# Two row-tile weighings moved from SBUF slots to PSUM banks, and a finer last product, in a fast matrix multiplication

## The chip, the cores and the metric

One core of one Trainium2 chip. The metric is device time in microseconds (us), the median over the executions of one kernel; 2% is the limit for calling two kernels different.

## The reference

```python
x: (8, 2048, 2048) float32      w: (2048, 2048) float32
cs   = np.cumsum(x, axis=1)
diff = cs - (cs shifted by one row, zero in front)      # = x again
return np.matmul(diff, w).astype(np.float32)
```

The differences of a running sum are x itself, so the work is one product of 16384 x 2048 by 2048 x 2048.

## The kernel before

The kernel takes four tiles of 128 rows as a group and saves matmuls by multiplying sums of blocks (Strassen's and Winograd's idea, on two levels), in fp16. Before it is narrowed to fp16, each row is *weighed*: ScalarE (ACT) sums the absolute values of the row, VectorE (DVE) makes a scale of the sum (`scale_of`), ACT narrows the row with it (`ready`), and a DMA transposes it (`turn`). TensorE (PE) accumulates products in PSUM; V, X, Y and Z are pairs of the eight banks ([128, 512] f32 each) that the kernel allocates there. ACT evicts a product to a slot of the SBUF pool C (`keep`) or DVE adds it to one (`add`); `put` stores a slot, 512 KB.

The ACTIVATE that sums also writes its elementwise result (128x2048 into c at L105, 128x512 into b at L553 in the profile below), which nobody needs. `weigh` lets it fall into a free slot of C; `weigh_in` into two idle PSUM banks, 512 columns at a time:

```python
def product(ps, a, b, first):        # 16 matmuls of 512 columns, L468
def product_in(ps, a, b, first):     # 4 matmuls, L479

def keep(dst, ps, scale):            # ACT, L497
    for c, p in pieces_of(dst, ps):
        after("act", lambda: nc.scalar.activation(c, p, COPY, scale=scale))

def add(dst, ps, scale):             # DVE, L502
    ...scalar_tensor_tensor(c, p, scale, c, MUL, ADD)

def weigh(t, slot):                  # one ACTIVATE of 2048 columns, L105
    xf = came.pop(t)
    m, _ = after("act", lambda: measure(xf, new_c(slot)))
    ...

def weigh_in(t, ps):                 # four ACTIVATEs of 512 columns, L553, and a reduce on DVE, L561
    for i in range(4):
        ...nc.scalar.activation(ps[i % 2], xf[:, ds(i * NB, NB)], ABS,
                                scale=1.0 / ROW, accum_out=m4[:, i : i + 1])
    after("dve", lambda: nc.vector.tensor_reduce(m, m4, AX.X, ADD))
```

`after` keeps the instructions of an engine in the order in which they were written. This is the end of the first group of this kind, and the start of the group after it (`second`), where the two weighings stand:

```python
def group_plain(g, X, Y, Z, V, a, b, c, d):   # the first group of this kind
    ...
    product(Z, S1, T1, True)
    ...
    weigh(h + 4, b); scale_of(h + 4); ready(h + 4); turn(h + 4)
    fetch_x(h + 5)
    weigh(g + 5, c)                # row tile 9
    scale_of(g + 5)
    C22 = new_c(d)
    keep(C22, Z, vh)               # TensorE needs this bank pair again
    product(X, A22g, T4, False)
    C21 = new_c(b)
    keep(C21, X, vg)
    ready(g + 5); turn(g + 5); put(C21, g + 1, 0)
    product(Y, A21h, T3, False)
    ...

def group(g, X, Y, Z, V, a, b, c, d):
    second = g == PLAIN + 4
    ...
    if second:
        product(X, A11g, B11, True)
    ...
    keep(C11g, X, ug)
    S3g = sums(g, S4g)
    if second:
        weigh(h + 1, c)            # row tile 11
        ready(h + 1)
        less_in(*in4)
    turn(h + 1)
    fetch_x(h + 4)
    product(Y, A11h, B11, True)
    if second:
        weigh_in(g + 4, V)
    keep(C11h, Y, uh)
    ...
```

The changed part of the end of the last group, `four_last`, stands in the diff.

Of the kernel before, what the change touches and what calls it, by code (L numbers as in the profile page):

```python
# [33 lines left out]
def kernel(  # L34
# [6 lines left out]
    nc = tc.nc  # L41
    P = 128
# [7 lines left out]
    NB = 512  # L50
# [18 lines left out]
    out2 = out.rearrange("b s d -> (b s) d")  # L69
# [23 lines left out]
    def bank(i):  # L93
        return psum.tile([P, NB], f32, name=f"b{i}")
# [8 lines left out]
    def measure(xf, waste):  # L103
        m = small.tile([P, 1], f32, name="m")
        return m, nc.scalar.activation(  # L105
            waste.bitcast(f16), xf, ABS, scale=1.0 / ROW, accum_out=m
        )
# [26 lines left out]
    def after(engine, ask):  # L134
        if engine in last:
            with tc.issue_after(last[engine].ins):
                said = ask()
        else:
            said = ask()
        last[engine] = said[-1] if isinstance(said, tuple) else said  # L140
        return said


    with tc.tile_pool(name="ring", bufs=7) as ring, tc.tile_pool(
# [81 lines left out]
        def here(h, r):  # L226
            return range(1 if h == 0 and r == PLAIN - 1 else 2)
# [14 lines left out]
        def put(c, rows, columns, queue=nc.gpsimd):  # L242
            return queue.dma_start(out2[rows, columns], c)
# [20 lines left out]
        ps = [[bank(2 * r + n) for n in here(0, r)] for r in range(PLAIN)]  # L264
# [10 lines left out]
        for ko in range(KO - KQ):  # L275
# [9 lines left out]
            if ko in turns:  # L285
                q, a = turns[ko]
# [19 lines left out]
        ps = [[bank(2 * r + n) for n in here(1, r)] for r in range(PLAIN)]  # L306
# [170 lines left out]
    def product_in(ps, a, b, first):  # L477
        for k in range(4):
            nc.tensor.matmul(  # L479
                ps, a[k], b[k], start=(first and k == 0), stop=(k == 3), skip_group_check=True  # L480
            )
# [8 lines left out]
    def pieces_of(dst, ps):  # L490
        if isinstance(ps, list):
            return [(dst[:, ds(n * NB, NB)], ps[n]) for n in range(2)]
        return [(dst, ps)]

    def keep(dst, ps, scale):
        for c, p in pieces_of(dst, ps):
            after("act", lambda: nc.scalar.activation(c, p, COPY, scale=scale))  # L497

    def add(dst, ps, scale):
        for c, p in pieces_of(dst, ps):  # L500
            after(
                "dve", lambda: nc.vector.scalar_tensor_tensor(c, p, scale, c, MUL, ADD)  # L502
            )
# [9 lines left out]
    def less(dst, p, q):  # L513
        for k in range(len(dst)):
            after("dve", lambda: nc.vector.tensor_tensor(dst[k], p[k], q[k], SUB))  # L515
# [10 lines left out]
    def new_c(slot):  # L526
        return cpool.tile([P, NH], f32, name=f"c{slot}")
# [9 lines left out]
    def weigh(t, slot):  # L537
        if t < END:
            xf = came.pop(t)
            m, _ = after("act", lambda: measure(xf, new_c(slot)))  # L540
            got[t] = m, None, xf


    def weigh_in(t, ps):
        if t < END:
            xf = came.pop(t)
            m = small.tile([P, 1], f32, name="m")
            m4 = small.tile([P, 4], f32, name="m4")
            for i in range(4):
                at = ds(i * NB, NB)  # L550
                after(
                    "act",
                    lambda: nc.scalar.activation(  # L553
                        ps[i % 2],
                        xf[:, at],
                        ABS,
                        scale=1.0 / ROW,
                        accum_out=m4[:, i : i + 1],
                    ),
                )  # L560
            after("dve", lambda: nc.vector.tensor_reduce(m, m4, AX.X, ADD))  # L561
            got[t] = m, None, xf
# [21 lines left out]
    def unit(t):  # L584
        u = small.tile([P, 1], f32, name="u")
        after("dve", lambda: nc.vector.tensor_scalar(u, got[t][0], uw, None, MUL))  # L586
        return u
# [59 lines left out]
    def group_plain(g, X, Y, Z, V, a, b, c, d):  # L647
        h = g + 2
        ug, uh = unit(g), unit(h)
        A11g, A12g = parts(g)  # L650
        A11h, A12h = parts(h)
        A21g, A22g = parts(g + 1)
        product(X, A11g, B11, True)
        for k in range(3):
            block(B22, 1, 1, k, "act")
        C11g = new_c(a)
        keep(C11g, X, ug)
        for k in range(3, KH):
            block(B22, 1, 1, k, "act" if k < 6 else "dve")
        product(V, A12g, B21, True)  # L660
        product(Y, A11h, B11, True)
        add(C11g, V, ug)
        put(C11g, g, 0)

        less(T3[:2], B22[:2], B12[:2])
        total(S1, A21g, A22g, ADD)
        product(Z, A12h, B21, True)
        weigh(h + 1, d)
        C11h = new_c(b)
        keep(C11h, Y, uh)  # L670
        total(S2, S1, A11g, SUB)
        less(T2[:4], B22[:4], T1[:4])
        scale_of(h + 1)
        vg = unit(g + 1)
# [3 lines that stand above are left out]
        less(T2[4:], B22[4:], T1[4:])  # L678
        product(V, S1, T1, True)
        C22 = new_c(d)  # L680
        keep(C22, V, vg)
        less(T3[2:3], B22[2:3], B12[2:3])
        total(S4g, A12g, S2, SUB)
        product(X, S2, T2, False)
        C12g = new_c(c)
        keep(C12g, X, ug)
        total(A21g, A11g, A21g, SUB)
        less(T3[3:], B22[3:], B12[3:])
        product(V, S4g, B22, False)
        A21h, A22h = parts(h + 1)  # L690
        vh = unit(h + 1)
        weigh(g + 4, a)
        product(X, A21g, T3, False)
        total(S1, A21h, A22h, ADD)
        total(S2, S1, A11h, SUB)
        add(C11h, Z, uh)
        put(C11h, h, 0)
        scale_of(g + 4)
        ready(g + 4)
        turn(g + 4)  # L700
        add(C12g, V, ug)
        put(C12g, g, 1)
        fetch_x(g + 5)
        product(Y, S2, T2, False)
        C12h = new_c(a)
        keep(C12h, Y, uh)
        add(C22, X, vg)
        put(C22, g + 1, 1)
        total(S4h, A12h, S2, SUB)
        less(T4, B21, T2)  # L710
        product(Z, S1, T1, True)
        total(A21h, A11h, A21h, SUB)
        weigh(h + 4, b)
        scale_of(h + 4)
        ready(h + 4)
        turn(h + 4)
        fetch_x(h + 5)
        weigh(g + 5, c)
        scale_of(g + 5)
        C22 = new_c(d)  # L720
        keep(C22, Z, vh)
# [3 lines that stand above are left out]
        ready(g + 5)  # L725
        turn(g + 5)
        put(C21, g + 1, 0)
        product(Y, A21h, T3, False)
        add(C22, Y, vh)
        put(C22, h + 1, 1)  # L730
        less_in(*in2)
        less_in3(*in2)
        product(Z, S4h, B22, False)
        add(C12h, Z, uh)
        put(C12h, h, 1)
        fetch_x(g + 8)
        less_in(*in3)
        product(Y, A22h, T4, False)
        C21 = new_c(c)
        keep(C21, Y, vh)  # L740
        put(C21, h + 1, 0)

    def group(g, X, Y, Z, V, a, b, c, d):
        h = g + 2
# [5 lines left out]
        q, e, y, z = banks  # L750
# [6 lines left out]
        keep(C11g, X, ug)  # L757
        S3g = sums(g, S4g)
        if second:
            weigh(h + 1, c)  # L760
            ready(h + 1)
            less_in(*in4)
        turn(h + 1)
# [9 lines left out]
        vg, vh = unit(g + 1), unit(h + 1)  # L773
# [4 lines left out]
        one, two, A2 = sums_in(A12g, A12h, S4h, S0)  # L778
# [34 lines left out]
        one, two, A3 = sums_in(S4g, S4h, S0, S3g)  # L813
# [11 lines left out]
        one, two, A4 = sums_in(A22g, A22h, S1, S2)  # L825
# [46 lines left out]
        def four_last():  # L872
            a11, a12, a22, s1, s2, s3, s4 = A4
            Q1, Q2, Q4, t11, Q3, t21, t22 = in4
            C21g, C21h = new_c(b), new_c(c)
            product_in(q, a11, t11, True)
            keep(C21g[:, :NB], q, vg)
            product_in(X[0], a12, t21, False)
            add(C21g[:, :NB], X[0], vg)
            product_in(X[1], s4, t22, False)  # L880
            keep(C21g[:, NB:], X[1], vg)
            product_in(e, s1, Q1, True)
            add(C21g[:, NB:], e, vg)
            keep(C21h[:, NB:], Y[1], vh)
            add(C21h[:, NB:], e, vh)
            product_in(q, s2, Q2, False)
            add(C21g[:, NB:], q, vg)
            put(C21g, g + 1, 0)
            product_in(Y[0], a22, Q4, False)
            keep(C21h[:, :NB], Y[0], vh)  # L890
            product_in(q, s3, Q3, False)
            for n in range(2):
                at = ds(n * NB, NB)
                add(C21h[:, at], q, vh)
                nc.scalar.dma_start(out2[ds((h + 1) * P, P), at], C21h[:, at])

        inner_product(A3, in3, banks, C12g, C12h, *u, between_3)
        put(C12h, h, 1)
# [9 lines left out]
    for g in range(PLAIN, END, 4):  # L908
        (group_plain if g == PLAIN else group)(g, *banks, *slots)
        a, b, c, d = slots  # L910
# [31 lines left out]
```

## Time and profile before

| | before |
|---|---|
| median of 3 executions (range), us | 1509.28 (1508.52 to 1510.85) |
| span of the profiled execution, us | 1507.3 |
| TensorE busy, us (matmuls) | 1490.6 (6911) |
| TensorE's waits for ACT at the first boundary, us | 1.32 + 0.20, later 0.78 |
| TensorE's wait for DVE at the end, us | 0.50 |

The prediction below shows the lines behind these numbers. Two more lines, from the page's table of the costliest groups, name the two ways of weighing. The columns: line, engine, operation, output and inputs with their shapes, count; then busy time in us and mean ns of one; then idle time just before them and what ended most of it.

```profile
L105 ACT ACTIVATE c<-fin 128x2048 f16<-128x2048 f32 x92 | 175.7, 1910 | 242.4 <-DMA out_dram<-c 220.5
...
L553 ACT ACTIVATE b<-fin 128x512 f32<-128x512 f32 x116 | 67.8, 585 | 14.5 <-DMA fin<-in_x_dram 14.5
```

The first line is the reason to try the change: 92 weighings into C stood idle for 220.5 us behind stores out of C. The second says what a weighing in PSUM waits for instead: nothing but the load of x.

### The profile page before, as it was taken

How to read it: one execution, taken by the hardware profiler on the slowest of the kernel's cores; microseconds unless marked ns; L12 is line 12 of the kernel's file. 1: busy time of each engine (PE TensorE's matmuls, PEld its weight loads, DVE VectorE, ACT ScalarE, POOL GpSimd, SP SyncE). 2: the span in 40 equal slices, each digit the busy share in tenths (PEclk: the TensorE clock that was granted, in tenths of full speed). 3: DMA queues.
4: the chain of work that ended last, by engine and by line, in shares of the span. 5: the costliest groups of instructions: out<-in, count | busy, mean ns of one | idle time of the engine just before them, and what ended most of it. 6: DMA issues, size and time to landing. Idle time of an engine off the chain costs nothing.

```text
span 1507.3 us, 19123 instructions
## 1 busy us (share of the span) xinstructions
PE 1490.6 (99%) x6911; PEld 673.8 (45%) x6911; DVE 1104.4 (73%) x2053; ACT 864.5 (57%) x1107; POOL 5.2 (0%) x12
## 2 busy tenths in 40 slices
PE   8999999999999999999999999999999999999998
PEld 3444444444444444444444444444444444444443
DVE  7997777776677676777676776766776767776767
ACT  5875655565655566555656555655555565556551
POOL 0100000000000000000000000000000000000000
PEclk9999999999999999999999999999999999999999
DMA  9988878878978987888789788878788888887772
GB/s 362 351 250 233 236 224 246 234 213 227 235 225 244 224 224 236 215 246 236 210 229 232 230 241 217 235 222 248 216 244 207 236 221 250 232 236 216 223 208 112
DMA packets 322479, 351.50 MB, mean 233 GB/s; under 512 B 266896, under 2 KB 266896, under 8 KB 306512
## 3 DMA queue, kind: packets, MB, share of 16 engines
q1 hardware_dynamic: 321536, 347.92, 81.1%
q0 software_dynamic: 560, 1.84, 0.3%
q8 instruction: 54, 0.88, 0.2%
q10 hardware_dynamic: 288, 0.52, 0.1%
q14 instruction: 41, 0.34, 0.1%
HBM read 150.99 MB, written 134.22 MB: 189 GB/s over the span
## 4 chain that ended last, share of the span: by engine, by line
PE 88%; DVE 1%; DMA 1%; issue 0%; ACT 0%; DVEq 0%; ACTq 0%; SPq 0%
PE b L468 52%; PE b L479 36%; DVE c L502 1%; DMA fin<-in_x_dram 0%; DMA xT<-fin 0%; DVE W L511 0%; ACT b L553 0%; DVE W L515 0%; ACT c L497 0%; DVEq L937 0%; DVE xT L511 0%; DVE s L112 0%; DVE m L111 0%; DVE u L586 0%; DVE m L561 0%
## 5 line engine op out<-in xcount | busy, mean ns | idle before, releaser
L502 DVE SCALAR_TENSOR_TENSOR c<-b,u,c 128x512 f32<-128x512 f32 (+1 forms) x883 | 675.0, 799 | 234.8 <-ACT c L497 112.8
L497 ACT ACTIVATE c<-b,u 128x512 f32<-128x512 f32 x496 | 314.5, 680 | 265.4 <-PE b L468 170.5
L468 PE MATMUL b<-W,xT 128*128 128x512 f16 x2048 | 462.1, 379 | 0.8 <-ACT c L497 0.8
L468 PE MATMUL b<-W,W 128*128 128x512 f16 x1764 | 411.7, 379 | 1.8 <-ACT c L497 1.5
L105 ACT ACTIVATE c<-fin 128x2048 f16<-128x2048 f32 x92 | 175.7, 1910 | 242.4 <-DMA out_dram<-c 220.5
L468 PEld LDWEIGHTS <-xT 128*128 128x128 f16 x2048 | 200.4, 98 | 242.6 <-issue 1.1
L468 PEld LDWEIGHTS <-W 128*128 128x128 f16 x2016 | 197.2, 98 | 240.2 <-issue 2.1
L116 ACT ACTIVATE fin<-fin,s 128x2048 f16<-128x2048 f32 x123 | 246.3, 2002 | 93.8 <-issue 50.8
L479 PEld LDWEIGHTS <-W 128*128 128x128 f16 x1560 | 152.1, 98 | 187.5 <-issue 2.5
L479 PE MATMUL b<-W,W 128*128 128x512 f16 x810 | 220.0, 379 | 1.0 <-DVE c L502 1.0
L479 PE MATMUL b<-W,xT 128*128 128x512 f16 x720 | 180.0, 379 | 0.0
L479 PE MATMUL b<-inner,W 128*128 128x512 f16 x660 | 176.2, 379 | 0.0
L479 PEld LDWEIGHTS <-xT 128*128 128x128 f16 x960 | 93.9, 98 | 113.3
L561 DVE TENSOR_REDUCE m<-m 128x1 f32<-128x4 f32 x29 | 4.6, 157 | 106.7 <-ACT b L553 106.7
L553 ACT ACTIVATE b<-fin 128x512 f32<-128x512 f32 x116 | 67.8, 585 | 14.5 <-DMA fin<-in_x_dram 14.5
L468 PE MATMUL b<-W 128*128 128x512 f16 x252 | 75.0, 379 | 0.0
L511 DVE TENSOR_TENSOR W<-W,xT 128x1024 f16<-128x1024 f16 x122 | 68.2, 559 | 3.2
L511 DVE TENSOR_TENSOR W<-xT,W 128x1024 f16<-128x1024 f16 x122 | 67.5, 553 | 0.0
L479 PE MATMUL b<-inner,xT 128*128 128x512 f16 x240 | 61.6, 379 | 0.0
L233 PE MATMUL b<-wb,xP 128*128 128x512 bf16 x240 | 55.4, 383 | 5.9 <-ACT wb L216 4.8
L511 DVE TENSOR_TENSOR W<-xT,xT 128x1024 f16<-128x1024 f16 (+1 forms) x92 | 54.8, 596 | 0.0
L111 DVE TENSOR_SCALAR m<-m 128x1 f32<-128x1 f32 x124 | 18.5, 149 | 34.6 <-ACT c L105 33.5
(54 smaller groups left out, 457.9 us busy)
## 6 DMA issues: line engine op xcount, KB each, us to landing
out_dram<-c SPq DMA_DIRECT2D x247, 512.0 KB, 3.1
fin<-in_x_dram SPq DMA_DIRECT2D x123, 1024.0 KB, 5.5
W<-in_w_dram SPq DMA_DIRECT2D x32, 512.0 KB, 9.6
W<-in_x_dram SPq DMA_DIRECT2D x16, 256.0 KB, 7.4
xT<-fin SPq DMA_TRANSPOSE x184, 5.2
out_dram<-o POOLq DMA_DIRECT2D x7, 256.0 KB, 3.9
out_dram<-o SPq DMA_DIRECT2D x7, 256.0 KB, 4.1
xP<-in_x_dram SPq DMA_DIRECT2D x1, 1024.0 KB, 5.1
```

The source lines that it names most:

```text
L105: return m, nc.scalar.activation(waste.bitcast(f16), xf, ABS, scale=1.0 / ROW, accum_out=m)
L111: nc.vector.tensor_scalar(m, m, TINY, None, MAX)
L116: return xh, nc.scalar.activation(xh, xf, COPY, scale=s)
L233: lambda: nc.tensor.matmul(ps[r][n], xP[:, r, ko, :], wb[h, ko][:, ds(n * NB, NB)], start=(ko == 0), stop=(ko == KO - 1),),
L468: nc.tensor.matmul(ps[n], a[k], b[k][:, n, :], start=(first and k == 0), stop=(k == KH - 1), skip_group_check=True,)
L479: nc.tensor.matmul(ps, a[k], b[k], start=(first and k == 0), stop=(k == 3), skip_group_check=True)
L497: after("act", lambda: nc.scalar.activation(c, p, COPY, scale=scale))
L502: "dve", lambda: nc.vector.scalar_tensor_tensor(c, p, scale, c, MUL, ADD)
L511: after("dve", lambda: nc.vector.tensor_tensor(dst.all, p.all, q.all, op))
L553: lambda: nc.scalar.activation(ps[i % 2], xf[:, at], ABS, scale=1.0 / ROW, accum_out=m4[:, i : i + 1],),
L561: after("dve", lambda: nc.vector.tensor_reduce(m, m4, AX.X, ADD))
```

## The change

Its intent: at the end of the first group, where every slot of C is in use, the two weighings shall not wait for a slot. And at the very end the last product is cut into two column halves, so that the last adds and stores are smaller.

```diff
@@ group_plain
         fetch_x(h + 5)
-        weigh(g + 5, c)
+        weigh_in(g + 5, V)
         scale_of(g + 5)
@@ group
         if second:
-            weigh(h + 1, c)
+            weigh_in(h + 1, V)
             ready(h + 1)
@@ four_last
             C21g, C21h = new_c(b), new_c(c)
+            def out_of(c, t, at, queue):
+                queue.dma_start(out2[ds(t * P, P), at], c[:, at])
             product_in(q, a11, t11, True)
             keep(C21g[:, :NB], q, vg)
             product_in(X[0], a12, t21, False)
             add(C21g[:, :NB], X[0], vg)
+            out_of(C21g, g + 1, ds(0, NB), nc.sync)
+            product_in(q, s2, Q2, False)
+            keep(C21g[:, NB:], q, vg)
+            product_in(e, s1, Q1, True)
+            one, two = (ds(n * NB // 2, NB // 2) for n in range(2))
+            keep(C21h[:, two], Y[0][:, two], vh)
+            keep(C21h[:, NB:], Y[1], vh)
             product_in(X[1], s4, t22, False)
-            keep(C21g[:, NB:], X[1], vg)
-            product_in(e, s1, Q1, True)
             add(C21g[:, NB:], e, vg)
-            keep(C21h[:, NB:], Y[1], vh)
             add(C21h[:, NB:], e, vh)
-            product_in(q, s2, Q2, False)
-            add(C21g[:, NB:], q, vg)
-            put(C21g, g + 1, 0)
-            product_in(Y[0], a22, Q4, False)
-            keep(C21h[:, :NB], Y[0], vh)
+            add(C21g[:, NB:], X[1], vg)
+            out_of(C21g, g + 1, ds(NB, NB), nc.sync)
             product_in(q, s3, Q3, False)
-            for n in range(2):
-                at = ds(n * NB, NB)
-                add(C21h[:, at], q, vh)
-                nc.scalar.dma_start(out2[ds((h + 1) * P, P), at], C21h[:, at])
+            keep(C21h[:, one], q[:, one], vh)
+            add(C21h[:, NB:], q, vh)
+            add(C21h[:, two], q[:, two], vh)
+            out_of(C21h, h + 1, ds(NB, NB), nc.scalar)
+            for at, ps, queue in (one, Y[0], nc.sync), (two, X[0], nc.scalar):
+                product_in(ps[:, at], a22, [b[:, at] for b in Q4], ps is X[0])
+                add(C21h[:, at], ps[:, at], vh)
+                out_of(C21h, h + 1, at, queue)
```

## The prediction

The forecast's sum for the end came to 0.9 us won. Of its terms only the 0.33 us for the smaller last store is left (128 KB less, at the 370 to 410 GB/s read from the profile), so that the 0.9 can't be added up from what remains. The paragraph without a heading gives costs from the profile before; its sentence on bank q can be seen in the trace of the changed kernel, where the eviction of 256 columns from q ends at 1502.73 us and the add waiting for it begins at 1502.76.

> **What bounds the kernel now.** I read the page first, then TensorE's waits, then the timeline around each wait, then the last microseconds.
>
> ```profile
> PE 1490.6 (99%) x6911; PEld 673.8 (45%) x6911; DVE 1104.4 (73%) x2053; ACT 864.5 (57%) x1107; POOL 5.2 (0%) x12
> ...
> PE b L468 <- ACT c L497: 2.3, 3, 1.3
> ...
> PE b L479 <- DVE c L502: 1.0, 3, 0.5
> ```
>
> TensorE is the bound and near its pace: in the chain of work 64 matmuls take 13.81 us, 215.8 ns each, and 6911 times 215.8 ns is 1491 us. Only 16.7 us of the span of 1507.3 lie outside and are left to win, most of them in the ramp of the first 25 us. The diff touches three places: two waits of TensorE for ScalarE (ACT) at the end of the first group, and what follows the last matmul.
>
> ```profile
> 115.76 1.91 ACT L105 ACTIVATE c<-fin 128x2048 f16<-128x2048 f32 x1 [1.94 <-DMA fin<-in_x_dram]
> ...
> 117.67 2.40 ACT L497 ACTIVATE c<-b,u 128x512 f32<-128x512 f32 x4
> ...
> 118.39 0.38 PE L468 MATMUL b<-W,W 128*128 128x512 f16 x1 [1.32 <-ACT c L497]
> ...
> 131.93 1.91 ACT L105 ACTIVATE c<-fin 128x2048 f16<-128x2048 f32 x1
> ...
> 136.31 0.58 ACT L553 ACTIVATE b<-fin 128x512 f32<-128x512 f32 x1
> ...
> 138.76 3.54 ACT L497 ACTIVATE c<-b,u 128x512 f32<-128x512 f32 x6
> ...
> 140.63 3.61 PE L468 MATMUL b<-W,xT 128*128 128x512 f16 x16 [0.78 <-ACT c L497]
> ```
>
> The reader should see two chains. In the first, ACT weighs row tile 9 (115.76), then evicts a PSUM tile (117.67), and TensorE needs that bank. The weighing started late, but its bracket names the load of x, not a store from the slot of C: the slot's store was asked at 106.84, the load only at 109.23. In the second, weighing tile 11 (131.93) starts the moment the eviction before it ends, without any wait; a narrowing, another weighing (in PSUM already, in four short ACTIVATEs) and six evictions of half a tile follow, and TensorE waits until 140.63 for the third of these. So in neither place does the slot of C hold anything up. What counts is how long ACT takes.
>
> ```profile
> 1499.28 2.07 DVE L502 SCALAR_TENSOR_TENSOR c<-b,u,c 128x512 f32<-128x512 f32 x3 [0.81 <-PE b L479]
> ...
> 1501.40 0.38 PE L479 MATMUL b<-W,W 128*128 128x512 f16 x1 [0.50 <-DVE c L502]
> ...
> 1502.53 1.41 DVE L502 SCALAR_TENSOR_TENSOR c<-b,u,c 128x512 f32<-128x512 f32 x2 [1.18 <-PE b L479]
> 1503.32 1.00 ACTq L895 DMA_DIRECT2D out_dram<-c  x2
> ```
>
> At the end TensorE waits once for VectorE (DVE) to empty a bank, then two adds and two stores of 256 KB follow. The DMA view of 1500 to 1508 us, in slices of 0.2 us, shows bytes flowing until about 1505.7 us, 1.6 us before the span ends.
>
> [...]1.91 us to the next instruction after the long weighing (115.76 to 117.67), 2.45 us for four short ones (136.31 to 138.76), 2.07 us for three adds. [...]in the changed kernel one DVE add of bank q waits for ACT's eviction from the same bank. [...]a 256 KB store lands in 2.4 us, with 370 to 410 GB/s while it flows.
>
> **Part one, tile 9 weighed in PSUM.** Removed: a 2048-wide ACTIVATE, 1.91 us to its successor. Added: four 512-wide ones, 2.45 us, and one TENSOR_REDUCE on DVE (157 ns in the page), which lies beside. The start stays at 115.76, since the load sets it. The eviction and TensorE behind it come 2.45 - 1.91 = **0.54 us later**: the wait of 1.32 becomes about 1.86.
>
> **Part two, tile 11.** Relative to that shift ACT is 0.54 us longer again, and the reduce stands in the chain to the scale that the narrowing waits for: 0.19 us more. So the evictions come 0.73 us later. But the built order moves three matmuls (0.65 us) ahead of the waiting product. Arrival of TensorE: 139.47 + 0.54 + 4 x 0.216 = 140.87; release: 140.63 + 0.54 + 0.73 = 141.90; wait 1.03. Afterwards three matmuls less remain: 141.90 + 16 x 0.216 = 145.35, against 140.63 + 19 x 0.216 = 144.73. Total shift 0.62, so this part costs **0.08 us**.
>
> **What follows.** The built order also puts three matmuls of the next product ahead of the one that starts DVE's long run at 148.29. The run then begins 0.65 us later beside TensorE; three other matmuls pulled forward fill the hole at 159.03 (0.20 wait), so that hole stays or shrinks by 0.1. The next one has no filler: at 168.54 the product with s4 has 0.5 us of slack against DVE's last sum (168.02), and DVE is 0.65 late: a new wait of **0.2 us**. Sum of the boundary: 0.54 + 0.08 + 0.2 - 0.1 = 0.7 us lost. The groups after it have no short waits before 629 us and keep the shift.
>
> **Part three, the end,** on the clock of before. Order of TensorE: q, X[0], then q with s2 at 1497.35 (it waits 0.06 for an eviction), e 1498.21, X[1] 1499.07, q with s3 1499.93, then eight 256-wide matmuls from 1500.79[...]. The wait of 0.50 is gone[...]. But DVE now sets the end. After 1498.47 it has seven adds[...]. Before, the last add ended at 1503.94[...]. The last store is 128 KB in place of 256 KB, 0.33 us less of flow[...]. Sum: **0.9 us won**.
>
> **Sum:** 1509.28 + 0.7 - 0.9 = 1509.1 us.
>
> **Rivals.** (a) The slots of C do hold the weighings up, as the change assumes, and PSUM frees them: both waits go, 2.3 us, and the end gives 0.9, so 1506 us. For it: other weighings of this kernel do wait for out_dram<-c, 220.5 us in sum in the page. Against it: these two do not, by their own rows. I give it 7%. (b) The lateness of ACT passes on whole, DVE's run stays late into the second group, or transfers shift so that the small wait at 651 us (0.3, behind a late load) grows: 1.5 us lost, 1510 us. For it: DVE has 0.7 us of idle from 118 to 137 us. Against: TensorE got filler. 20%. (c) The end wins nothing, as seven adds on DVE take the place of the wait and small stores cost as much as large ones: 1510 us.[...] 13%. (d) The end wins more, 1.5 us, if 256-wide instructions are cheaper than I take them: 1508.5. 15%.
>
> **Range and chances.** The three runs before spread over 2.3 us, more than any term of my sum; a median of three may be off by 0.7. With 0.6 for the terms, I take 1507.8 to 1510.4. All that the change touches is under 8 us of 1509, and 2% are 30 us: within 2% is as good as certain, 0.99; the rest is shared.
>
> **What would show it.** Right: four short weighings with accumulators at about 115.8, the wait of TensorE near 118.9 grown to about 1.9; near 141.9 a wait of about 1.0; near 169 a new one of 0.2; TensorE's wait for ACT in sum about 3.1 us instead of 2.3; matmul work the same but for four more instructions; no wait of 0.5 at the end, DVE the engine before the last store[...]. Wrong: weighings that start earlier than before, which speaks for (a); TensorE's wait for DVE in the second group above 0.7 us, which speaks for (b); a last store that lands as late as before, which speaks for (c).

## The result, and the profile after

| | before | changed |
|---|---|---|
| median of 3 executions (range), us | 1509.28 (1508.52 to 1510.85) | 1509.88 (1508.90 to 1510.08) |
| span of the profiled execution, us | 1507.3 | 1508.1 |
| ratio to before, 95% interval | | 1.0000 (0.9978 to 1.0023) |

A ratio here is the mean time of one kernel's fast executions over the mean of the other's from the same rounds, so it is not quite the ratio of the medians. The result is correct (`again` below, the same kernel, has it on record).

First the page of the changed kernel, the line of the engines and the two ways of weighing:

```profile
PE 1492.8 (99%) x6915; PEld 674.3 (45%) x6915; DVE 1105.4 (73%) x2057; ACT 866.1 (57%) x1120; POOL 5.0 (0%) x12
...
L105 ACT ACTIVATE c<-fin 128x2048 f16<-128x2048 f32 x90 | 171.9, 1910 | 245.1 <-DMA out_dram<-c 228.5
...
L553 ACT ACTIVATE b<-fin 128x512 f32<-128x512 f32 x124 | 72.6, 586 | 14.4 <-DMA fin<-in_x_dram 13.9
```

Two weighings left C and eight short ones came to PSUM, as meant. But ACT's idle time behind stores out of C is not smaller, it is 228.5 us where it was 220.5. That fits what the prediction read from the brackets of the two rows, that neither waited for a store; the sum alone would not show it. TensorE has four matmuls more. Of its 2.2 us more of busy time, 1.8 lie in the ramp, in a group of 240 matmuls (L233) that took 55.4 us before and 57.2 here, ahead of every edit.

TensorE's waits, in us in total, times, and the longest:

```profile
PE b L468 <- ACT c L497: 2.7, 3, 1.6
...
PE b L479 <- DVE c L502: 0.4, 1, 0.4
```

The waits for ACT grew from 2.3 to 2.7; those for DVE shrank from 1.0 to 0.4: the 0.5 at the end is gone, the 0.2 at 159 us has fallen below the 0.15 us from which this view counts, and the one at 651 us is 0.36 where it was 0.33. The timeline of the changed kernel at the first boundary (start, length, engine, line, operation, tiles, count, and in brackets the idle time before with what ended it):

```profile
116.09 0.60 ACT L553 ACTIVATE b<-fin 128x512 f32<-128x512 f32 x1 [1.70 <-DMA fin<-in_x_dram]
...
118.55 2.39 ACT L497 ACTIVATE c<-b,u 128x512 f32<-128x512 f32 x4
...
119.27 0.38 PE L468 MATMUL b<-W,W 128*128 128x512 f16 x1 [1.63 <-ACT c L497]
...
140.35 1.03 PE L479 MATMUL b<-W,xT 128*128 128x512 f16 x4
...
142.20 3.61 PE L468 MATMUL b<-W,xT 128*128 128x512 f16 x16 [0.83 <-ACT c L497]
```

The bracket of the weighing of tile 9 names the load of x as before: the bank frees nothing here. From the start of the weighing to the eviction are 118.55 - 116.09 = 2.46 us, which were 117.67 - 115.76 = 1.91. TensorE waits 1.63 us in place of 1.32. At the second place four matmuls now stand ahead of the wait (140.35), and the wait is 0.83 in place of 0.78.

The end of the changed kernel:

```profile
1496.80 1.89 PE L479 MATMUL b<-W,xT 128*128 128x512 f16 x8
...
1500.60 4.09 DVE L502 SCALAR_TENSOR_TENSOR c<-b,u,c 128x512 f32<-128x512 f32 x7 [0.89 <-PE b L479]
...
1502.05 1.04 PE L479 MATMUL b<-inner,xT 128*128 128x256 f16 x8
1503.54 1.51 ACTq L878 DMA_DIRECT2D out_dram<-c  x2
```

No wait of TensorE is left, and DVE runs its last seven adds in one piece. To compare ends, I count from the row of eight matmuls (the products with a11 and a12) that opens the end in both kernels, at 1496.80 here; I call it the start of the end. In the kernel before it is

```profile
1495.56 1.89 PE L479 MATMUL b<-W,xT 128*128 128x512 f16 x8
```

From there the last add ends after 8.39 us before and 7.89 in the changed kernel, and the span ends after 11.78 and 11.31: **0.47 us won**, though 0.50 were won by the last add alone.

For the boundary, the change shows best if TensorE's matmuls are counted. I took matmul 488 (at about 110 us, ahead of every edit) as the common point, and read how much later than before the matmuls 520, 600, 660, 720 and 800 start, and the first one of the end. Matmul 520 lies behind the first wait, 660 behind the second, 720 behind the small hole at 159 us, 800 at about 180 us. (In most traces some six records of the ramp are missing; I counted from the end.)

| us later than before | 520 | 600 | 660 | 720 | 800 | start of the end |
|---|---|---|---|---|---|---|
| changed kernel | 0.31 | 0.31 | 0.36 | 0.29 | 0.48 | 0.67 |

So the changed kernel loses 0.48 us at the boundary and another 0.19 in the 1300 us after it, and wins 0.47 at the end. And matmul 488 itself came at 110.57 where it came at 110.00 before, which is no work of the change. The sum, 0.57 + 0.67 - 0.47 = 0.77 us, is the difference of the two spans, 0.8. In the twelve profiles matmul 488 lies between 109.82 and 110.61: the ramp alone has a noise as large as anything that the change does.

### The profile page after: what moved, and what is told of

Read it like the earlier page. It is cut to its first block, busy times and chain, and to the rows that moved or that the text cites. A ratio compares the mean times of both kernels' runs of the same rounds, so it can differ in the third digit from the quotient of the medians.

```text
span 1508.1 us, 19151 instructions
## 1 busy us (share of the span) xinstructions
PE 1492.8 (99%) x6915; PEld 674.3 (45%) x6915; DVE 1105.4 (73%) x2057; ACT 866.1 (57%) x1120; POOL 5.0 (0%) x12
## 3 DMA queue, kind: packets, MB, share of 16 engines
q0 software_dynamic: 560, 1.84, 0.3%
## 4 chain that ended last, share of the span: by engine, by line
PE 88%; DVE 1%; DMA 1%; ACT 0%; issue 0%; DVEq 0%; ACTq 0%; SPq 0%
PE b L468 52%; PE b L479 35%; DVE c L502 1%; DMA fin<-in_x_dram 0%; DMA xT<-fin 0%; DVE W L511 0%; DVE W L515 0%; ACT c L497 0%; ACT b L553 0%; DVEq L947 0%; DVE xT L511 0%; DVE s L112 0%; DVE m L111 0%; DVE u L586 0%; DVE m L561 0%
## 5 line engine op out<-in xcount | busy, mean ns | idle before, releaser
L502 DVE SCALAR_TENSOR_TENSOR c<-b,u,c 128x512 f32<-128x512 f32 (+2 forms) x885 | 675.4, 798 | 233.2 <-ACT c L497 112.5
L497 ACT ACTIVATE c<-b,u 128x512 f32<-128x512 f32 (+1 forms) x497 | 315.1, 680 | 263.9 <-PE b L468 169.6
L105 ACT ACTIVATE c<-fin 128x2048 f16<-128x2048 f32 x90 | 171.9, 1910 | 245.1 <-DMA out_dram<-c 228.5
L553 ACT ACTIVATE b<-fin 128x512 f32<-128x512 f32 x124 | 72.6, 586 | 14.4 <-DMA fin<-in_x_dram 13.9
L233 PE MATMUL b<-wb,xP 128*128 128x512 bf16 x240 | 57.2, 392 | 5.2 <-ACT wb L216 3.9
L479 PE MATMUL b<-inner,xT 128*128 128x512 f16 (+1 forms) x244 | 61.6, 376 | 0.0
L511 DVE TENSOR_TENSOR xT<-xT,xT 128x1024 f16<-128x1024 f16 x62 | 42.6, 688 | 1.0
```

Of the source, the lines that this page charges most:

```text
L105: return m, nc.scalar.activation(waste.bitcast(f16), xf, ABS, scale=1.0 / ROW, accum_out=m)
L233: lambda: nc.tensor.matmul(ps[r][n], xP[:, r, ko, :], wb[h, ko][:, ds(n * NB, NB)], start=(ko == 0), stop=(ko == KO - 1),),
L479: nc.tensor.matmul(ps, a[k], b[k], start=(first and k == 0), stop=(k == 3), skip_group_check=True)
L502: "dve", lambda: nc.vector.scalar_tensor_tensor(c, p, scale, c, MUL, ADD)
L511: after("dve", lambda: nc.vector.tensor_tensor(dst.all, p.all, q.all, op))
L553: lambda: nc.scalar.activation(ps[i % 2], xf[:, at], ABS, scale=1.0 / ROW, accum_out=m4[:, i : i + 1],),
```

## The experiments

Ten kernels ran; the kernel before ran beside them (medians 1509.28, 1509.43 and 1509.99 us). Kernels are compared only within the same rounds. All are correct. The table by stages, one profile each, with the changed kernel for comparison:

| kernel | 520 | 600 | 660 | 720 | 800 | start of the end to last add | start of the end to span's end |
|---|---|---|---|---|---|---|---|
| before | 0 | 0 | 0 | 0 | 0 | 8.39 | 11.78 |
| changed | 0.31 | 0.31 | 0.36 | 0.29 | 0.48 | 7.89 | 11.31 |
| tail_only | -0.06 | -0.06 | -0.06 | -0.06 | -0.06 | 7.89 | 11.29 |
| end_whole | -0.05 | -0.05 | 0.10 | 0.10 | 0.10 | 7.59 | 11.42 |
| end_sems | 0.14 | 0.14 | 0.14 | 0.14 | 0.14 | 7.89 | 10.94 |
| weigh_only | 0.47 | 2.15 | 1.08 | 1.01 | 1.20 | 8.38 | 11.79 |
| weigh9_only | 0.17 | 0.16 | 0.16 | 0.16 | 0.16 | 8.38 | 11.79 |
| weigh11_only | -0.06 | -0.06 | 0.01 | -0.06 | 0.13 | 8.38 | 11.78 |
| again | 0.38 | 2.06 | 0.99 | 0.92 | 1.11 | 7.89 | 11.30 |
| evict_first | -0.82 | 1.48 | 1.97 | 1.90 | 1.91 | 7.89 | 11.30 |
| evict_early | -1.48 | -1.42 | 1.89 | 1.52 | 1.53 | 7.89 | 11.31 |
| early_banks | -1.48 | -1.84 | -0.81 | -1.17 | -1.17 | 7.89 | 10.95 |

The three kernels that leave the boundary alone (tail_only, end_whole, end_sems) differ by 0.2 us in these columns, so one or two tenths mean little and a half means something.

### The end: tail_only, end_whole, end_sems

**tail_only** has the new end and the old weighings.

> The kernel before with the new end alone. My theory: nothing differs up to the last five products; the wait of 0.5 us in the end goes, TensorE ends 0.57 us sooner after the start of the last products than in the kernel before, the last add of DVE 0.5 us sooner, and the span ends 0.4 to 0.9 us sooner from the same mark; ratio 0.9994 to 0.9998. The rival (small stores take the gain back): the span ends within 0.2 us of the kernel before from the same mark, ratio 1.0000.

Measured: 1509.28 us (1507.93 to 1509.56), ratio 0.9999 (0.9986 to 1.0011). The stages show what the times cannot: nothing lost at the boundary, 11.78 - 11.29 = 0.49 us won at the end.

**end_whole** is tail_only with the last product in one piece again:

```diff
-            keep(C21h[:, two], Y[0][:, two], vh)
...
-            keep(C21h[:, one], q[:, one], vh)
+            keep(C21h[:, :NB], q, vh)
             add(C21h[:, NB:], q, vh)
-            add(C21h[:, two], q[:, two], vh)
             out_of(C21h, h + 1, ds(NB, NB), nc.scalar)
-            for at, ps, queue in (one, Y[0], nc.sync), (two, X[0], nc.scalar):
-                ...
+            keep_whole = ds(0, NB)
+            product_in(Y[0], a22, Q4, False)
+            add(C21h[:, keep_whole], Y[0], vh)
+            out_of(C21h, h + 1, keep_whole, nc.sync)
```

> The new end with the last product in one piece of 512 columns, one add and one store of 256 KB in place of halves; old weighings. If the gain of the end comes from the new order of products, which takes the wait away, this ends as soon as the halves: the last add of DVE some 0.3 us sooner than with halves (two adds of 512 in place of one of 512 and three of 256), its store 0.3 us longer, the end within 0.2 us. If it is the smaller stores that gain, the end is 0.4 us or more later than with halves.

Measured: 1509.11 us (1508.23 to 1509.63), ratio 0.9998 (0.9986 to 1.0011). The end of DVE's work, in its timeline:

```profile
1501.56 1.41 DVE L502 SCALAR_TENSOR_TENSOR c<-b,u,c 128x512 f32<-128x512 f32 x2 [0.31 <-ACT c L497]
```

Two whole adds end DVE's work 7.59 us after the start of the end, 0.30 sooner than the halves do, yet the span ends 11.42 after it, 0.13 later. So the new order of the products brings 11.78 - 11.42 = 0.36 us of the gain, and the halves with their smaller last store only 0.13. About 0.06 of that is no work of the store: in end_whole the last landing is on semaphore 100 and seven closing waits follow it, in tail_only six (see the next run).

**end_sems** asks where the rest of the expected 0.9 us went. In the raw records, SyncE ends the program with a series of waits on DMA semaphores, in rising order, about 0.06 us each if the transfer is done, and then drains:

```
before     1505.689 on 108   1506.462 on 109   drain 1506.527
tail_only  1505.748 on 100   1506.091 on 102   1506.156 on 103   1506.217 on 104
           1506.276 on 105   1506.338 on 106   1506.397 on 108   1506.459 on 109   drain 1506.524
end_sems   1505.921 on 108   1506.306 on 109   drain 1506.371
```

Before, the last two stores had the last two semaphores of the row. In the new end they have 100 and 102, and six further waits follow the last landing: 1506.459 - 1506.091 = 0.37 us. The edit splits the stores of the last group, so that the count of DMAs is another and the last two stores fall on 108 and 109:

```diff
     def put(c, t, h):
-        after("sp", lambda: nc.sync.dma_start(out2[ds(t * P, P), ds(h * NH, NH)], c))
+        parts_of = 2 if t >= END - 4 else 1
+        n = NH // parts_of
+        for i in range(parts_of):
+            after("sp", lambda: nc.sync.dma_start(
+                out2[ds(t * P, P), ds(h * NH + i * n, n)], c[:, ds(i * n, n)]))
```

> The new end alone, with six earlier stores of the last group cut in two, so that twelve DMAs stand where six stood and the two last stores of 128 KB fall on the last two of the eight DMA semaphores in turn, as the last two stores of the kernel before did. In the traces SyncE's closing waits go through the semaphores in a fixed order, some 0.061 us each; with the new end alone the last store landed with six waits still to go. Theory: those six waits (0.37 us) are what is missing of my 0.9 us, so from the start of the last eight products of the four-matmul kind to the end of the span it takes 10.9 us, against 11.26 with the new end alone and 11.74 before. Rival: the small stores themselves land later than I took them to, and this ends at 11.2 to 11.3 like the new end alone.

Measured: 1508.96 us (1507.59 to 1509.65), ratio 0.9994 (0.9982 to 1.0007). The last add still ends after 7.89 us, and the span after 10.94: 0.35 us sooner than tail_only. The earlier stores of the group are smaller here too, but the last store lands no sooner for it: 10.06 us after the start of the end, against 10.03 in tail_only (landings in the raw records, 1506.289 and 1506.075). So the closing waits are the cause of the missing part.

### The boundary: weigh_only, weigh9_only, weigh11_only, again

**weigh_only** has both weighings in PSUM and the old end, **weigh9_only** and **weigh11_only** have one each; their edits are the first two hunks of the diff above, both or one of them. **again** is the changed kernel itself, with five executions.

> The kernel before with both weighings in PSUM and the old end. My theory (ACT time, not the slots of C, sets the two waits, and the longer weighings make them worse): TensorE is 0.5 to 0.7 us later at 170 us than in the kernel before when both are set to the same start of the matmul stream at 107 us; the first wait is 0.3 to 0.6 us longer than before, the second about 1.0 after three matmuls more, a new wait of about 0.2 stands near 169 us; the total is 0.3 to 0.9 us slower, ratio 1.0002 to 1.0006. The rival (the slots hold the weighings up): both waits go, total 2 us faster, ratio 0.9987.

> Only tile 9 is weighed in PSUM, all else as before; the built order of TensorE is that of the kernel before. Theory: the first wait for ACT grows by 0.54 us less or plus what the load of x arrives earlier or later (0.3 to 0.8 in all), the second wait stays near 0.8 and the one near 159 us near 0.2, since all of ACT, DVE and TensorE shift together; total 0.3 to 0.8 us slower. Rival (slot of C): first wait gone, total 1.3 us faster.

> Only tile 11 is weighed in PSUM. Theory: the first wait stays at 1.3 plus 0.2, the second is 0.9 to 1.1 after four short matmuls in place of one, and near 169 us there is a new gap of about 0.2; TensorE is some 0.3 us later at 170 us than in the kernel before. Rival (slot of C): the second wait gone, 0.8 us faster.

> The changed kernel once more, as it is, against five rounds of the kernel before. My theory (0.5 lost at the boundary, 0.5 won at the end, and in some executions a stretch at half clock after the longer first wait, 1.7 us): median 0 to 0.8 us slower than before, ratio 1.0000 to 1.0005; the waits for ACT 1.4 to 2.1 us at 119 us, 0 to 1.0 at 142, the end from the start of the last eight products 11.2 to 11.4 us. Rival (the change gains): 0.5 us or more faster.

| | median (range), us | ratio to before (95%) |
|---|---|---|
| weigh_only | 1510.02 (1509.76 to 1512.19) | 1.0008 (0.9994 to 1.0022) |
| weigh9_only | 1510.51 (1509.62 to 1510.98) | 1.0006 (0.9993 to 1.0018) |
| weigh11_only | 1509.53 (1509.07 to 1511.12) | 1.0002 (0.9989 to 1.0014) |
| again | 1509.82 (1509.41 to 1511.09) | 1.0002 (0.9988 to 1.0015) |

None is faster. Rival (a) would have made weigh_only some 2 us faster, which its interval excludes; for one weighing alone (0.8 to 1.3 us) the waits decide. The first is still there in weigh9_only, the second in weigh11_only:

```profile
119.05 0.38 PE L468 MATMUL b<-W,W 128*128 128x512 f16 x1 [1.48 <-ACT c L497]
```

```profile
141.47 3.61 PE L468 MATMUL b<-W,xT 128*128 128x512 f16 x16 [0.82 <-ACT c L497]
```

In the five profiles with the old weighing of tile 9 and the old order (before, tail_only, end_whole, end_sems, weigh11_only) the first wait is 1.25 to 1.46 us, in the four with the new one (changed, again, weigh_only, weigh9_only) 1.48 to 1.79. So the weighing of tile 9 costs TensorE 0.17 to 0.47 us there, the lowest no more than end_sems has without it (0.14); the mean of the waits grows by 0.34. That of tile 11 costs next to nothing at the second wait (from -0.06 to 0.01 at matmul 660 in weigh11_only), and it alone brings the 0.19 us between 720 and 800: that step is in changed, again, weigh_only and weigh11_only, and not in weigh9_only. Two expectations were too high: weigh9_only's first wait grew by 0.16, not 0.3 to 0.8, and weigh11_only was 0.13 us late near 170 us, not 0.3. The later part of weigh11_only is inconclusive: in its profile TensorE waits 1.1 us more between 800 and 1480 us, in one execution and in none of the others that share its edit.

One thing nobody expected: weigh_only and again lose 1.7 us between matmul 520 and 600, where no wait is. In weigh_only's timeline, around its first wait:

```profile
119.46 0.38 PE L468 MATMUL b<-W,W 128*128 128x512 f16 x1 [1.79 <-ACT c L497]
120.04 1.93 PE L468 MATMUL b<-W,W 128*128 128x512 f16 x5 [0.20 <-ACT c L497]
```

Five matmuls take 1.93 us; in the kernel before a row of five like it takes 1.24. The view of windows tells why. It gives the busy time of each engine with its instructions (PE, PEld for TensorE's weight loads, DVE, ACT, POOL), then PEclk, the granted clock of TensorE as a share of the full one, then the DMA engines' busy share and GB/s. First weigh_only, then the changed kernel's first profile:

```profile
120.00:122.00 2.00, 1.96 (x6) 0.78 (x6) 2.00 (x6) 2.00 (x3) 0.00 (x0) 0.61 0.63 172
122.00:124.00 2.00, 2.00 (x6) 0.69 (x5) 2.00 (x7) 1.03 (x1) 0.00 (x0) 0.54 0.85 356
```

```profile
120.00:122.00 2.00, 2.00 (x10) 0.88 (x9) 2.00 (x7) 2.00 (x3) 0.00 (x0) 1.00 0.78 242
122.00:124.00 2.00, 2.00 (x11) 0.93 (x10) 2.00 (x8) 0.84 (x1) 0.00 (x0) 1.00 0.68 287
```

TensorE has six matmuls at work in two microseconds instead of ten or eleven. The clock records put the granted clock at 0.5 for 3.413 us in weigh_only (120.4 to 123.9 us) and in again (119.9 to 123.3), and never there in the kernel before or in the first profile of the changed kernel. Half speed for 3.413 us loses 1.7 us (2.15 - 0.47 = 1.68 between matmuls 520 and 600 in weigh_only, 2.06 - 0.38 = 1.68 in again); 1.07 of it come back by matmul 660 (2.06 to 0.99 in again), because TensorE then arrives late at the second place and finds nothing to wait for (no wait of TensorE is listed between 125 and 157 us in again).

The traces also show what came before it. In each of the twelve, the clock changes lie whole multiples of 3.413 us after the first change (438 in the kernel before and 437 in the changed kernel, to the half clock near the end of the span; 32 and 33 in weigh_only, 30 and 31 in again, 37 and 38 in evict_early below), so each trace gives its own grid of steps. On it, by the records of its matmuls, TensorE stood idle for 1.98 us (weigh_only), 1.89 (again) and 2.37 (evict_early) of the step just before the half clock began. In no other step between the first clock change and 1490 us of any trace was it idle for more than 1.82 us (the changed kernel, at its first wait), and no other step was followed by half clock. So in these traces 1.89 us of idle time and more in one step was followed by half clock, and 1.82 and less was not. In evict_first below a gap of 1.98 us is cut into 1.44 and 0.54 by the grid, and nothing follows. As waits in the view of time, 1.69 + 0.20 us (again), 1.79 + 0.20 (weigh_only) and 2.17 + 0.20 (evict_early), with one matmul between the two parts, were followed by half clock; 1.63 + 0.20 (the first profile of the changed kernel), 1.98 alone (evict_first) and 1.38 + 0.20 (early_banks) were not.

How often it strikes can only be guessed from the mean granted clock of each execution, which is given to three places; 3.413 us at half lower it by 0.001. All 27 executions of the kernel before, and all 25 of tail_only, end_whole, end_sems, weigh11_only and early_banks, read 0.999 or 1.000. Of the 18 executions in which tile 9 is weighed in PSUM behind the old order (the changed kernel, again, weigh_only, weigh9_only) six read 0.998, among them the two with the records; evict_first and evict_early have one each of five. So it may strike about every third time; only the three in records are shown.

### Taking the waits away: evict_first, evict_early, early_banks

If not the slot but ACT's order makes TensorE wait, evicting ahead of weighing must take the first wait away, with no bank at all. Both kernels have the new end and the old weighings.

**evict_first** moves the eviction ahead of the weighing, and does the like for the second place:

```diff
-        weigh(g + 5, c)
-        scale_of(g + 5)
         C22 = new_c(d)
         keep(C22, Z, vh)
+        weigh(g + 5, c)
+        scale_of(g + 5)
...
-        if second:
-            weigh_in(g + 4, V)                    # ahead of keep(C11h, Y, uh)
...
         keep(C12g, X, ug)
+        if second:
+            reduce = weigh_in(g + 4, V, later=True)
...
         add(C12g, Z, ug)
+        if second:
+            reduce(); scale_of(g + 4)
```

> The new end, the old weighings in slots of C, and two evictions by ACT moved ahead of the weighings that they waited behind. If ACT's order and time set the two waits, as I hold, both go (1.5 and 0.8 us), some 0.2 may come back as a wait near 159 or 169 us, and with the end the total is 2 to 3 us faster than before, ratio 0.998 to 0.9987. If the waits are set by something else (the slot of C that the eviction itself needs, the arrival of x), the first wait stays above 1 us and the total is within 1 us of the new end alone.

Measured: 1510.46 us (1510.19 to 1511.82), ratio 1.0011 (0.9998 to 1.0024): a miss. Its timeline:

```profile
116.64 1.26 ACT L497 ACTIVATE c<-b,u 128x512 f32<-128x512 f32 x2 [3.01 <-DMA out_dram<-c]
117.38 0.38 PE L468 MATMUL b<-W,W 128*128 128x512 f16 x1 [0.50 <-ACT c L497]
...
133.84 0.61 PE L468 MATMUL b<-W,W 128*128 128x512 f16 x2 [1.98 <-DVE W L511]
...
149.35 0.59 PE L479 MATMUL b<-W,W 128*128 128x512 f16 x2 [1.30 <-DVE c L502]
```

The first wait falls to 0.50 and the second is gone, but the eviction now waits 3.01 us for a store from its own slot of C, and the weighing comes after it. DVE has the scale of tile 9 at the head of its work, begins it at 119.83 us and works without a pause up to the sums that begin at 132.38; TensorE waits 1.98 us for the sum that follows, and 1.30 us later on. The waits moved to DVE.

**evict_early** evicts into the slot that is free sooner, moves two sets of DVE's subtractions ahead of the scale, and weighs into the other slot:

```diff
-        weigh(g + 5, c)
-        scale_of(g + 5)
-        C22 = new_c(d)
+        C22 = new_c(c)
         keep(C22, Z, vh)
+        less_in(*in2)
+        less_in3(*in2)
+        weigh(g + 5, d)
+        scale_of(g + 5)
...
-        less_in(*in2)
-        less_in3(*in2)
...
-        C21 = new_c(c)
+        C21 = new_c(d)
...
-        slots = (b, d, a, c) if g == PLAIN else (a, d, b, c)
+        slots = (b, c, a, d) if g == PLAIN else (a, d, b, c)
```

> New end alone plus a new order at the boundary: the eviction that TensorE waits for first goes into the slot of C whose store landed 5 us earlier, and runs in the idle time of ACT before tile 9 arrives; sixteen subtractions of DVE that do not need tile 9 move ahead of its scale. Theory (ACT's and DVE's order behind the late load of tile 9 is what both waits come from): the first wait (1.3 plus 0.2) and the second (0.8) both go, TensorE is 2 to 2.5 us earlier at 180 us, total 2.3 to 3 us faster than before, 1506.5. Rival (tile 9's load, its transposition and the sums on it bind whatever the order): a wait of 1 to 2 us for DVE's sums appears near 131 us, as in the run with the evictions moved ahead, and the total is within 1 us of the new end alone.

Measured: 1509.57 us (1508.56 to 1510.94), ratio 0.9998 (0.9984 to 1.0011): a miss, 1506.5 was expected. Its timeline:

```profile
117.02 1.91 ACT L105 ACTIVATE c<-fin 128x2048 f16<-128x2048 f32 x1 [1.90 <-DMA out_dram<-c]
...
131.84 1.91 ACT L105 ACTIVATE c<-fin 128x2048 f16<-128x2048 f32 x1 [2.69 <-DMA out_dram<-c]
...
140.53 0.38 PE L468 MATMUL b<-W,xT 128*128 128x512 f16 x1 [2.17 <-ACT c L497]
141.11 5.08 PE L468 MATMUL b<-W,xT 128*128 128x512 f16 x15 [0.20 <-ACT c L497]
```

The first wait for ACT is gone, and TensorE is 1.48 us early at matmul 520. But now both weighings do what the change had feared: they wait 1.90 and 2.69 us for stores out of C. The second wait grows to 2.17 us, and the half clock follows it (15 matmuls in 5.08 us; the records have 0.5 for 3.413 us from 141.7 us). From matmul 600 to 660 it loses 3.31 us: 2.37 of waiting instead of 0.78, and 1.7 for the clock. Here the banks would have something to free.

**early_banks** is evict_early with both weighings in PSUM, as the change has them, and with the stores of end_sems:

```diff
-        weigh(g + 5, d)
+        weigh_in(g + 5, V)
...
-            weigh(h + 1, c)
+            weigh_in(h + 1, V)
```

> The order of the run with the eviction moved early, with both weighings in PSUM as the change has them, and the new end with its last stores on the last two semaphores. In that earlier run both weighings waited 1.9 and 2.7 us for stores from slots of C, once the first wait was gone. Theory: PSUM takes just these two waits away: ACT starts weighing tile 9 when its load has landed (near 115.5) and tile 11 straight after the eviction before it (near 129); TensorE's waits between 107 and 157 us are under 0.6 us in sum (2.3 in the kernel before), no stretch at half clock follows; from 107 us of TensorE's stream to 180 us it is some 1.8 to 2.3 us shorter than in the kernel before, the end 0.8; total 2.3 to 3.1 us faster, ratio 0.998 to 0.9985. Rival (a next link of the chain takes the place of the removed one: DVE, the loads): the waits move to another line and the total is within 1 us of before.

Measured: **1507.71 us** (1507.05 to 1509.47), ratio to before 0.9989 (0.9976 to 1.0001); the changed kernel had 1509.82 and the kernel before 1509.99. Its timeline:

```profile
115.72 0.60 ACT L559 ACTIVATE b<-fin 128x512 f32<-128x512 f32 x1 [0.43 <-DMA fin<-in_x_dram]
...
128.14 1.27 ACT L497 ACTIVATE c<-b,u 128x512 f32<-128x512 f32 x2 [2.76 <-DMA out_dram<-c]
129.29 0.60 ACT L559 ACTIVATE b<-fin 128x512 f32<-128x512 f32 x1
...
139.49 0.38 PE L468 MATMUL b<-W,xT 128*128 128x512 f16 x1 [1.38 <-ACT c L497]
```

Tile 9 is weighed when its x is there, and tile 11 right behind the eviction, 2.55 us sooner than in evict_early. TensorE is 1.17 us ahead of before at matmul 800 and the end is 11.78 - 10.95 = 0.83 us shorter: 2.0 us by these two stages, 1.5 by the whole spans, 2.3 by the medians. The median and both stages are ahead of both kernels, but the interval reaches 1.0001, so the gain in time is not clear of the noise. It is less than was expected (ratio 0.998 to 0.9985, waits under 0.6 us in sum): a wait of 1.38 + 0.20 us is left, and an eviction that waits 2.76 us for a slot; those were not tried further. What the banks themselves bring is less than the step from evict_early suggests: of the 2.70 us between the two at matmul 800, 1.7 are the half clock that struck in the one profile of evict_early and not in this one, so about 1.0 is left (though that clock itself followed the long wait that the banks shorten); and of the end, 0.36 us belong to the stores of end_sems. No run has this order with the weighings in C, these stores and the full clock.

## Why the prediction was right

The time was 1509.88 us, inside the range and 0.8 above the point. That says little by itself: the range is wider than all that the change does, and the kernel before, 1509.28 us, lies in it too. The stages are the test. The profiled execution is the one of 1509.88 us, and its ramp was 0.57 us later than that of before. By stages it lost 0.48 us at the boundary and 0.19 after it and won 0.47 at the end, where the prediction had 0.7 lost and 0.9 won. So both sizes were too large, and in the sum they partly cancelled: 0.2 us won were forecast, 0.2 lost were measured, and neither is clear of the noise.

- **Bound and size.** Right: TensorE's pace is the time (1490.6 us busy of 1507.3), and what the change touches is worth less than a microsecond. Two readings there were off, and no term rests on them: of the 16.7 us outside TensorE's work only 5.6 lie in the first 25 us and as much as 5.4 in the last 17 (view of windows), and DVE's idle time from 118 to 137 us, given for rival (b), is 1.0 us, not 0.7.
- **Part one.** The step "0.54 us later" is right: 2.46 - 1.91 = 0.55. The wait became 1.63, not 1.86, since in that execution the load ended ACT's idle time after 1.70 us and not after 1.94. The assumption that the start stays put was the loose part: 0.31 lost here, 0.38 in again, 0.47 in weigh_only, 0.17 in weigh9_only.
- **Part two.** Predicted 0.08 us with a wait of 1.03; measured 0.05 (inside the noise) with a wait of 0.83. That TensorE would find matmuls to do ahead of the wait was the deciding observation.
- **What follows.** The hole at 159 us shrank by 0.07 (predicted 0.1 at most), and the new gap took 0.19 (predicted 0.2). Boundary in sum 0.48, predicted 0.7; the difference is the load of part one.
- **Part three.** The steps of DVE's chain rested on costs of 256-column instructions that no trace had shown then; that DVE would set the end was right. In the changed kernel its seven adds begin 3.80, 4.53, 5.20, 5.96, 6.63, 7.02 and 7.41 us after the start of the end, and the last is done after 7.89, where it was 8.39 before: 0.50 us won. For the whole end 0.9 were forecast and 0.47 measured. Of the terms one is left, "The last store is 128 KB in place of 256 KB, 0.33 us less of flow". The store did land sooner: SyncE's wait for it ended 1506.091 - 1496.04 = 10.05 us after the start of the end in tail_only, against 1506.462 - 1495.56 = 10.90 before, 0.85 us, of which 0.50 are the last add. But SyncE then still had six waits to go through, 0.37 us, so 0.48 was left: the sum lacked the term of the closing waits. For the same reason the span ended 1508.1 - 1503.09 = 5.0 us after the last matmul, no sooner than before (1507.3 - 1502.42 = 4.9).
- **Rival (a)**, the slot of C as the true wait, fell for the kernel as it was, by the bracket at 116.09 and by weigh_only, which is not faster. evict_early showed that it holds as soon as the first wait is gone.
- **Rival (b)** fell in its own form: the small wait at 651 us went from 0.33 to 0.36 and no more. But lateness did have a price that neither the sum nor a rival named, the half clock: with it (again), the boundary costs 1.11 us instead of 0.48.
- **Rivals (c) and (d)**: the end won 0.47, between the two. What the prediction took the 256-column instructions to cost was not shown by the profile before. Measured, adds of 256 columns begin every 0.39 us (raw records of tail_only and of the changed kernel) where those of 512 begin every 0.66 (1497.65 to 1498.97 in the changed kernel); the record of an eviction of 256 columns is 0.47 us (1501.49 in tail_only), 0.22 less than the 0.69 of one of 512; and matmuls of 256 columns begin every 0.109 us (1502.05 to 1502.82 in the changed kernel), where those of 512 take 0.216.

Open: how often the half clock strikes, and whether there is a sharp limit between the 1.82 us that were not followed by it and the 1.89 that were; how much of early_banks' gain the banks bring; and whether the extra waits of weigh11_only were more than one odd execution.

## What to carry to other kernels

Before freeing a resource, look at the bracket of the very instructions concerned: 220 us of idle time for a cause in the whole page say nothing about the two rows that one edit touches, and weighing in four short pieces cost ACT 0.55 us for each tile, whether or not it saved a wait. Then ask what is next in line: the same two weighings that lost 0.5 us here were worth about 1 us, by the profiles, once the eviction went first. And the time of a last store is not the end of a program: look at what follows its landing.
